# A streaming-encoder block on one core: the second up-projection phase as one chunk of 1024 tokens with halves of 512 columns, weights loaded and right factors built in the stages before

## The chip, the cores and the metric

The kernel runs on one core of a Trainium2 chip. The metric is the device time of one execution in microseconds. A core has TensorE (PE; its weight loads are listed apart as PEld), VectorE (DVE), ScalarE (ACT), GpSimd (POOL) and SyncE (SP), which here issues all DMAs in one queue. Every engine works its instructions off in a fixed order, and a waiting instruction holds up what stands behind it on its engine.

## What is computed

One layer on 2048 tokens of width 1024 with 16 learned meta tokens ahead of them: a norm, one input projection for two head groups (stick-breaking attention and a gated recurrence), one output projection with a residual, and then the part that the change touches:

```python
hn2 = rmsnorm(h, norm2_g[layer])
ug = causal_dwconv(hn2 @ w_ffn_in[layer], ffn_conv_w[layer], ffn_conv_b[layer])
u, g = jnp.split(ug, [D_FF], axis=-1)
h = h + (jax.nn.silu(g) * u) @ w_ffn_out[layer]
```

`w_ffn_in` is 1024 x 5632, `w_ffn_out` 2816 x 1024, all in float32. Each float32 factor is split in a rounded high part and the remainder, and a product is three matmuls (high by high, high by low, low by high).

## The kernel before

**Stages.** The program goes through the input projection and the recurrence, then attention, then stage C (`token_tile` and `turn2`, 17 steps: output projection, residual, second norm, transpose; the normed tokens are written to the DRAM tensor `hnT`), and stage D. Stage D goes over the tokens in two phases of 1024. In each phase `ffn_in(jf, ph)` is called for the 22 tiles `jf` of 128 columns of both halves of `w_ffn_in`, and its gated result is stored in `pd`; then `ffn_out(q)` is called for two quarters of 512 tokens, each over the 22 tiles of `w_ffn_out`, with eight accumulators in the eight PSUM banks.

**ffn_in.** The up-projection of a chunk is a 2 x 2 block product by a scheme with seven products in place of eight. Left factors: `weights(jf)` loads two tiles `wst`, forms four sums on DVE (lines 836 to 839) and splits seven factors: the high part by a copy on ACT, the low part by a subtraction on POOL (`split`, lines 704 and 705). They lie in nine rotating buffers `wt`. Right factors: `build(ch, kk, ...)` loads four blocks of `hnT` (line 717), forms four differences on DVE (line 719) and splits seven blocks into `bH` and `bL`, both on ACT and DVE. A chunk is 512 tokens, so that its blocks have 256 columns (258 in the first chunk, which has a halo of four tokens); two chunks are worked side by side, each with banks X, V and Y, and `both` runs every product for one chunk and then for the other. A product is 4 x 3 matmuls (line 851). Copies on ACT (`snap`, line 873) and additions on DVE (`plus`, line 879) make the results from the banks; then come the convolution, the gate, and a DMA to `pd` (lines 897 to 911).

**Where factors are made.** The factors of the first chunk are built during stage C (line 802), those of the second chunk at the start of stage D, those of the third and fourth between `ffn_out(1)` and the second phase (lines 941 and 942). The staging tiles of a build are the tiles `c0` and `c1` (two buffers each), which are also the results of `ffn_in` and the output rows of `ffn_out`. `wst` (four buffers) belongs to the pool of stage D.

**Order.** The tile framework simulates the program as it is written and sets each engine's order by that, so that work of one call can stand among that of the calls around it.

Of the kernel before, what the change touches and what calls it, by code (L numbers as in the profile page):

```python
# [16 lines left out]
P = 128  # L17
META = 16
# [3 lines left out]
KD = D // P  # L22
HEADS = 8
HD = 64
NT = SEQ // P
DFF = 2816
KF = DFF // P
# [4 lines left out]
HALO = 4  # L32
CHW = 512
PHW = 2 * CHW
# [21 lines left out]
def hymba_block(  # L56
# [650 lines left out]
    def half_of(ch):  # L707

        return (META - HALO, (CHW + HALO) // 2) if ch == 0 else (META + ch * CHW, CHW // 2)

    def build(ch, kk, mp, tmp):

        c0, nh = half_of(ch)
        b0, b1 = tmp()
        bt = [t[:, c * nh:(c + 1) * nh] for t in (b0, b1) for c in range(4)]
        for n, a, h in ((B11, 0, 0), (B12, 0, 1), (B21, 1, 0), (B22, 1, 1)):
            nc.sync.dma_start(bt[n], hnT[:, kk + 4 * a, c0 + h * nh:c0 + (h + 1) * nh])  # L717
        for o, a, b in ((T1, B12, B11), (T3, B22, B12), (T2, B22, T1), (T4, B21, T2)):
            nc.vector.tensor_tensor(bt[o], bt[a], bt[b], op=ALU.subtract)  # L719
        H = mp.tile([P, 7, (CHW + HALO) // 2], F32R, name=f"bH{ch % 2}{kk}", tag=f"bH{kk}")[:, :, :nh]  # L720
        L = mp.tile([P, 7, (CHW + HALO) // 2], F32R, name=f"bL{ch % 2}{kk}", tag=f"bL{kk}")[:, :, :nh]
        for d0, d1, t, m in ((0, 4, b0, 4), (4, 7, b1, 3)):
            split(H[:, d0:d1], L[:, d0:d1], t[:, :m * nh].rearrange("p (m t) -> p m t", m=m), nc.vector)
        return H, L

    with ExitStack() as CD:
        up = pool(CD, "up", 1, side="right")
        edge = up.tile([P, 2 * KF, 2], F32, name="edge")
        mats = [[], []]

        with ExitStack() as C:
            C.enter_context(ps_tu)
# [59 lines left out]
            for i in range(NT + 1):  # L792
                if 0 < i < NT:
                    mixed(i + 1)
                if i == 0:
                    g2b = cp.tile([P, D], F32, name="g2b", bufs=1)
                hg = token_tile(i, *((mA, mB)[i % 2] if i else (mM, None)), g2b)
                if late:
                    turn2(*late)
                late = (i, hg)  # L800
                if i in (8, 10, 12, 14):
                    mats[0].append(build(0, i // 2 - 4, up, ctmp))
            turn2(*late)
        wo_stack.close()

# [7 lines left out]
        with ExitStack() as Dx:  # L813
# [10 lines left out]
            def dtmp():  # L824
                return [ctile(a) for a in range(2)]

            def weights(jf):

                wu, wg = [dp.tile([P, KD, P], F32, name="wst", tag="wst", bufs=4) for e in range(2)]
                for e, w in ((0, wu), (1, wg)):  # L830
                    m = e * KF + jf
                    nc.sync.dma_start(w, w_f[:, m * P:(m + 1) * P].rearrange("(k p) c -> p k c", p=P))
# [12 lines left out]
                return out  # L845
# [9 lines left out]
            def ffn_in(jf, ph):  # L855
                a11, s1, s2, s4, s3, a12, a22 = weights(jf)
                cu, cg = ctile(0), ctile(1)
                sides = []
                for c in range(2):
                    nh = half_of(2 * ph + c)[1]  # L860
                    x0 = 0 if ph + c == 0 else HALO + c * CHW
                    sides.append((nh, slice(x0, x0 + nh), slice(x0 + nh, x0 + 2 * nh)))
                X, V, Y = [[bank()[:, :sides[c][0]] for c in range(2)] for _ in range(3)]

                def both(ps_, wt, b, first):
                    for c in range(2):
                        product(ps_[c], wt, mats[c], b, first)

                def snap(ps_, name):
                    out = []  # L870
                    for c in range(2):
                        t = dp.tile([P, (CHW + HALO) // 2], F32, name=f"{name}{c}", tag=f"{name}{c}", bufs=1)
                        nc.scalar.copy(t[:, :sides[c][0]], ps_[c])
                        out.append(t[:, :sides[c][0]])
                    return out

                def plus(dst, s, ps_, sb):
                    for c in range(2):
                        nc.vector.tensor_tensor(dst[:, sides[c][s]], ps_[c], sb[c], op=ALU.add)

                both(X, a11, B11, True)
                p1 = snap(X, "p1")
# [11 lines left out]
                for c in range(2):  # L894
                    nc.scalar.copy(cg[:, sides[c][1]], X[c])
# [17 lines left out]
            def ffn_out(q):  # L913

                acc = [[bank() for e in range(2)] for i in range(4)]
                for jf in range(KF):
                    st = dp.tile([P, KD, P], F32, name="wst", tag="wst", bufs=4).rearrange("p k c -> p (k c)")
                    nc.sync.dma_start(st, w_fo[jf * P:(jf + 1) * P, :])
                    oH, oL, pp = [dp.tile([P, 2, 4, P], F32R, name="wt", tag="wt", bufs=9) for _ in range(3)]
                    oH, oL = [t.rearrange("p a k c -> p (a k c)") for t in (oH, oL)]  # L920
                    split(oH, oL, st, nc.gpsimd)
                    pt = dp.tile([P, PHW], F32, name="t", tag="t")[:, :512]
# [25 lines left out]

_INS = ["x", "meta_tokens", "norm1_g", "w_in", "q_norm_g", "k_norm_g", "conv_w", "conv_b",
# [20 lines left out]
```

## Time and profile before

| | |
|---|---|
| median of 3 runs | 2766.45 us (2764.97 to 2766.52) |
| the profiled execution | 2765.91 us, its span 2764.2 us |
| mean granted clock of TensorE, share of full speed | 0.976 |
| PE busy | 2580.0 us (93%) |
| PEld, DVE, ACT, POOL busy | 87%, 68%, 45%, 42% |
| matmuls of the up-projection (line 851) | 7392 |
| matmuls of the down-projection (lines 108 to 110, bank `bk`) | 2112 |

The span is the time from the first to the last record. The execution's own time is 1.7 us more. A busy share is an average over stages with different limits. Matmuls are pipelined, so their durations overlap: how fast PE goes is read from how many start in a stretch, and where it stops from the idle time that stands in brackets behind a row, with the engine or transfer that ended it. The granted clock is given as a share of full speed, 1.00 for 2.4 GHz and 0.50 for 1.2 GHz.

### The profile page before, as it was taken

Reading aid. Unit: us, or ns where it says so; the run is one execution under the profiler, and the core shown is the slowest. Engines: PE = TensorE matmul, PEld = TensorE weight load, DVE = VectorE, ACT = ScalarE, POOL = GpSimd, SP = SyncE. Lnnn points to the kernel's source line nnn. Section 1 sums busy time; section 2 is a strip of 40 time slices with the busy share of each in tenths; the row PEclk is TensorE's granted clock in tenths of the full one; section 3 lists DMA queues with packets and bytes.
Section 4 is the critical chain, followed back from the end, with each engine's and each line's share of the span. In section 5 each row is a group of like instructions: output and inputs, shape, how many; then the busy total and the mean of one; then the engine's idle time right before and its main releaser. Section 6 shows DMA issues by size and latency. Waiting matters only on the chain.

```text
span 2764.2 us, 44289 instructions
## 1 busy us (share of the span) xinstructions
PE 2580.0 (93%) x16860; PEld 2392.4 (87%) x16860; DVE 1879.9 (68%) x2162; ACT 1250.4 (45%) x2419; POOL 1162.5 (42%) x1152
## 2 busy tenths in 40 slices
PE   7999799988888888999799999999969999999999
PEld 7998799977787778788699999988859999998887
DVE  5588843269999999564687777645458677765454
ACT  4355532246666667332345454432235454543222
POOL 4455564445433220000455555344436555553443
PEclk9999999999999999999899999999989999999999
DMA  4301133243333321575422222255442222224463
GB/s 154 110 32 38 47 110 99 77 111 111 94 80 80 80 72 50 162 221 181 118 92 70 85 77 78 95 171 202 152 149 77 78 76 81 81 77 160 147 204 115
DMA packets 319179, 296.64 MB, mean 107 GB/s; under 512 B 62438, under 2 KB 273622, under 8 KB 318966
## 3 DMA queue, kind: packets, MB, share of 16 engines
q1 hardware_dynamic: 318966, 293.82, 34.9%
q8 instruction: 132, 2.16, 0.3%
q14 instruction: 81, 0.66, 0.1%
HBM read 211.68 MB, written 82.07 MB: 106 GB/s over the span
## 4 chain that ended last, share of the span: by engine, by line
PE 47%; DVE 2%; POOL 1%; issue 1%; DMA 1%; SPq 0%; ACT 0%; POOLq 0%; DVEq 0%; ACTq 0%
PE bk L851 30%; PE bk L108 6%; PE bk L109 6%; PE bk L110 6%; POOL wt L705 1%; DMA out_dram<-c 0%; DMA wst<-in_w_ffn_in_dram 0%; DVE c L719 0%; DVE ss L837 0%; SPq L717 0%; DMA t<-pd 0%; DVE bL L705 0%; DVE ss L838 0%; DVE t L906 0%; DMA c<-hnT 0%
## 5 line engine op out<-in xcount | busy, mean ns | idle before, releaser
L851 PE MATMUL bk<-bH,wt 128*128 128x256 f32 (+1 forms) x4928 | 894.2, 284 | 37.9 <-ACT bH L704 18.3
L851 PEld LDWEIGHTS bk<-bH,wt 128*128 128x128 f32 x4928 | 767.4, 191 | 41.6 <-ACT bH L704 19.8
L851 PE MATMUL bk<-bL,wt 128*128 128x256 f32 (+1 forms) x2464 | 697.6, 284 | 4.9 <-DVE bL L705 4.9
L705 POOL TENSOR_TENSOR wt<-wst,wt 128x512 fp32r<-128x512 f32 (+1 forms) x264 | 464.6, 1762 | 398.0 <-ACT wt L704 388.0
L851 PEld LDWEIGHTS bk<-bL,wt 128*128 128x128 f32 x2464 | 469.8, 191 | 6.0 <-DVE bL L705 6.0
L704 ACT CAST wt<-wst 128x512 fp32r<-128x512 f32 (+1 forms) x264 | 201.4, 766 | 565.3 <-issue 301.9
L705 DVE TENSOR_TENSOR wt<-t,wt 128x512 fp32r<-128x512 f32 x88 | 202.8, 2307 | 228.0 <-ACT wt L704 228.0
L705 POOL TENSOR_TENSOR wt<-ss,wt 128x512 fp32r<-128x512 f32 x132 | 205.0, 1556 | 233.7 <-ACT wt L704 224.7
L108 PE MATMUL bk<-wt 128*128 128x512 f32 x704 | 275.5, 393 | 10.0 <-ACT wt L704 10.0
L109 PE MATMUL bk<-wt 128*128 128x512 f32 x704 | 276.0, 392 | 0.0
L110 PE MATMUL bk<-wt 128*128 128x512 f32 x704 | 271.6, 389 | 0.0
L580 DVE TENSOR_TENSOR_SCAN kp<-kp 128x456 f32<-128x456 f32 (+6 forms) x144 | 238.5, 1657 | 0.9
L612 PE MATMUL v<-tL,dv 128*128 128x256 f32 (+1 forms) x648 | 178.9, 301 | 43.2 <-DVE tL L586 42.0
L571 ACT ACTIVATE kp<-m 128x388 f32<-128x388 f32 (+13 forms) x360 | 169.1, 508 | 70.3 <-PE m L570 39.6
L906 DVE SCALAR_TENSOR_TENSOR t<-c,fw,t 128x1024 f32<-128x1024 f32 x88 | 132.5, 1506 | 78.3 <-ACT t L905 78.3
L612 PEld LDWEIGHTS v<-tL,dv 128*128 128x128 f32 x648 | 125.7, 194 | 58.9 <-DVE tL L586 57.2
L108 PEld LDWEIGHTS bk<-wt 128*128 128x128 f32 x704 | 133.6, 190 | 38.3 <-ACT wt L704 10.4
L908 DVE SCALAR_TENSOR_TENSOR c<-c,fw,t 128x1024 f32<-128x1024 f32 x88 | 160.5, 1824 | 3.0
L109 PEld LDWEIGHTS bk<-wt 128*128 128x128 f32 x704 | 133.6, 190 | 27.6
L110 PEld LDWEIGHTS bk<-wt 128*128 128x128 f32 x704 | 132.2, 188 | 27.6
L569 PE MATMUL m<-K,q 128*128 128x452 f32 (+12 forms) x360 | 143.1, 399 | 2.5 <-ACT kp L571 2.2
L563 POOL MEMSET kp<- 128x112 f32 x128 | 23.6, 190 | 284.9 <-PE t L97 130.8
(302 smaller groups left out, 5745.0 us busy)
## 6 DMA issues: line engine op xcount, KB each, us to landing
wst<-in_w_ffn_in_dram SPq DMA_DIRECT2D x88, 512.0 KB, 4.0
wst<-in_w_ffn_out_dram SPq DMA_DIRECT2D x88, 512.0 KB, 3.9
pd<-c SPq DMA_DIRECT2D x44, 512.0 KB, 2.7
t<-pd SPq DMA_DIRECT2D x88, 256.0 KB, 3.5
q<-qd SPq DMA_DIRECT2D x128, 128.0 KB, 2.8
wst<-in_w_in_dram SPq DMA_DIRECT2D x48, 192.0 KB, 2.7
xt<-in_x_dram SPq DMA_DIRECT2D x16, 512.0 KB
od<-qn SPq DMA_DIRECT2D x128, 64.0 KB, 2.1
```

What stands on the lines that cost most here:

```text
L108: nc.tensor.matmul(ps, lhsT=sH, rhs=mH, start=first, stop=False)
L109: nc.tensor.matmul(ps, lhsT=sH, rhs=mL, start=False, stop=False)
L110: nc.tensor.matmul(ps, lhsT=sL, rhs=mH, start=False, stop=last)
L569: nc.tensor.matmul(zt[:rn, :sz], lhsT=q2[:, 0, qc:qc + rn], rhs=K2[:, c0:c0 + sz], start=True, stop=False)
L571: nc.scalar.activation(kp[:rn, c0:c0 + sz], zt[:rn, :sz], AF.Sigmoid, scale=-0.125)
L580: nc.vector.tensor_tensor_scan(rev, rev, rev, initial=kp[:rn, hi:hi + 1], op0=ALU.mult, op1=ALU.bypass)
L612: nc.tensor.matmul(av[:, q0:q0 + nn], lhsT=dv[:pp, s].rearrange("p a d -> p (a d)"), rhs=tt[:pp, c:c + nn], start=(s == 0 and half == 0), ...
L704: nc.scalar.copy(h, src)
L705: low.tensor_tensor(l, src, f(h), op=ALU.subtract)
L851: nc.tensor.matmul(ps_, lhsT=s, rhs=m, start=first and k == 0 and n_ == 0, stop=k == 3 and n_ == 2, skip_group_check=True)
L906: nc.vector.scalar_tensor_tensor(t, c_[:, HALO - 1:HALO - 1 + PHW], pf[:, 1:2], t, op0=ALU.mult, op1=ALU.add)
L908: nc.vector.scalar_tensor_tensor(c_[:, uv], c_[:, uv], pf[:, 0:1], t, op0=ALU.mult, op1=ALU.add)
```

## The change

The second phase becomes one chunk of 1024 tokens whose blocks have 512 columns, with one set of banks X, V, Y: half as many matmuls, each twice as wide. The first phase keeps its two chunks. All right factors lie in two tiles, `mb0` and `mb1`, as large as before; in the second phase each holds two of the four `kk`. They are built during `ffn_out(1)`: `between(jf)` calls a build at the tiles 2, 6, 10 and 14. A build there uses all four buffers of `c0` and `c1`. `wst` moves to a pool that is open from stage C on, and the weights of the first two tiles are loaded in stage C. In the first tile of the first phase all work of the first chunk is written ahead of that of the second. `wt` has ten buffers in place of nine. The seven products, the convolution and the down-projection stay.

```diff
+    HW0 = (CHW + HALO) // 2
+    PHASES = (((META - HALO, HW0), (META + CHW, CHW // 2)), ((META + PHW, CHW),))
...
+        H, L = store
+        for n, t in enumerate(bt):
+            m = min(7 - n * per, per)
+            d = slice(n * per * nh, (n * per + m) * nh)
+            split(H[:, d], L[:, d], t[:, :m * nh], nc.vector)
...
+        wst = pool(CD, "wst", 1, side="right")
+        mb = [up.tile([P, 8 * 7 * HW0], F32R, name="mb0")]
...
+                if i == NT:
+                    staged = [stage_in(jf) for jf in range(2)]
...
-                    wt = dp.tile([P, 2, 4, P], F32R, name="wt", tag="wt", bufs=9)
+                    wt = dp.tile([P, 2, 4, P], F32R, name="wt", tag="wt", bufs=10)
...
-                X, V, Y = [[bank()[:, :sides[c][0]] for c in range(2)] for _ in range(3)]
+                X, V, Y = [[bank()[:, :s_[0]] for s_ in sides] for _ in range(3)]
+
+                apart = ph == 0 and jf == 0
+                queue = []
+
+                def run(job):
+                    for c in range(len(sides)):
+                        if apart:
+                            queue.append((c, job))
+                        else:
+                            job(c)
...
-            for ph in range(2):
-                if ph:
-                    mats[0] = [build(2, kk, up, dtmp) for kk in range(4)]
-                mats[1] = [build(2 * ph + 1, kk, up1, dtmp) for kk in range(4)]
-                for jf in range(KF):
-                    ffn_in(jf, ph)
-                for q in range(2):
-                    ffn_out(2 * ph + q)
+            mb.append(up1.tile([P, 8 * 7 * CHW // 2], F32R, name="mb1"))
+            mats[1] = [right(mb[1], PHASES[0][1], kk, 4) for kk in range(4)]
+            for jf in range(KF):
+                ffn_in(jf, 0, staged.pop(0) if staged else stage_in(jf))
+            ffn_out(0, [], lambda jf: None)
+            mats[0] = []
+
+            def between(jf):
+                if jf in (2, 6, 10, 14):
+                    kk = len(mats[0])
+                    mats[0].append(right(mb[kk // 2], PHASES[1][0], kk, 2))
+
+            ffn_out(1, [], between)
+            for jf in range(KF):
+                ffn_in(jf, 1, stage_in(jf))
+            for q in (2, 3):
+                ffn_out(q, [], lambda jf: None)
```

**What it moves in the engines' orders.** DVE at the start of stage D. `sT` is the last transposed tile of stage C, `ss` the sums of the weights, `c` a staging tile of the builds, `bL` the low parts of right factors. Before:

```order
L785 COPY sT<-u 128x512
L719 TENSOR_TENSOR c_14745<-c_14746,c_14745 128x256
L719 TENSOR_TENSOR c_14746<-c_14745,c_14746 128x256
L719 TENSOR_TENSOR c_14746<-c_14745 128x256
L719 TENSOR_TENSOR c_14746<-c_14745,c_14746 128x256
L719 TENSOR_TENSOR c_14761<-c_14762,c_14761 128x256
L705 TENSOR_TENSOR bL_14756<-c_14745,bH_14755 128x4x256
```

And with the change:

```order
L812 COPY sT<-u 128x512
L861 TENSOR_TENSOR ss<-wst 128x512
L862 TENSOR_TENSOR ss<-ss,wst 128x512
L864 TENSOR_TENSOR wst<-wst 128x512
L863 TENSOR_TENSOR ss<-wst,ss 128x512
L720 TENSOR_TENSOR c_14750<-c_14751,c_14750 128x256
L720 TENSOR_TENSOR c_14751<-c_14750,c_14751 128x256
```

The sums of the first tile's weights now stand ahead of the builds of the second chunk; before they stood behind eleven instructions of the builds.

DVE in `ffn_out(1)`, after the accumulators of `ffn_out(0)` have been read out. `wt<-t` is the low part of a tile from `pd`, one per `jf`; `mb` holds right factors. Before, 18 of these stood in one row:

```order
L705 TENSOR_TENSOR wt<-t,wt 128x512 x18
```

And with the change:

```order
L705 TENSOR_TENSOR wt<-t,wt 128x512 x2
L705 TENSOR_TENSOR mb_13216<-c_20868,mb_13216 128x1024
L720 TENSOR_TENSOR c_20869<-c_20871,c_20868 128x512
L705 TENSOR_TENSOR wt<-t,wt 128x512
L720 TENSOR_TENSOR c_20870<-c_20869,c_20871 128x512
L720 TENSOR_TENSOR c_20870<-c_20869 128x512
L705 TENSOR_TENSOR mb_13216<-c_20869,mb_13216 128x1024
L720 TENSOR_TENSOR c_20871<-c_20868,c_20870 128x512
L705 TENSOR_TENSOR mb_13216<-c_20870,mb_13216 128x1024
L705 TENSOR_TENSOR mb_13216<-c_20871,mb_13216 128x512
L705 TENSOR_TENSOR wt<-t,wt 128x512
```

This is the first of four builds; the 32 instructions of all four stand within seven steps of `jf`.

PE in the second phase, with the change. `bk_21982`, `bk_21983` and `bk_21984` are X, V and Y of the third tile, `bk_21840` and `bk_22124` X of the second and the fourth:

```order
L876 MATMUL bk_21982<-mb1_14749,wt_21959 128x512 x5
L876 MATMUL bk_21983<-mb0_13216,wt_21962 128x512 x6
L876 MATMUL bk_21983<-mb1_14749,wt_21962 128x512 x6
L876 MATMUL bk_21984<-mb0_13216,wt_21974 128x512 x6
L876 MATMUL bk_21984<-mb1_14749,wt_21974 128x512 x4
L876 MATMUL bk_21840<-mb0_13216,wt_21835 128x512 x6
L876 MATMUL bk_21840<-mb1_14749,wt_21835 128x512 x6
L876 MATMUL bk_21982<-mb0_13216,wt_21965 128x512 x6
L876 MATMUL bk_21982<-mb1_14749,wt_21965 128x512 x6
L876 MATMUL bk_21983<-mb0_13216,wt_21968 128x512 x6
L876 MATMUL bk_21983<-mb1_14749,wt_21968 128x512 x6
L876 MATMUL bk_21984<-mb1_14749,wt_21974 128x512 x2
```

Between the first product into X of a tile and the second one there are now products into V and Y and the last product of the tile before; each has 12 matmuls of 512 columns where two groups of 12 with 256 columns stood.

## Rows read from the trace of the kernel before

**Rows 1.** The page: the span, and the busy time of each engine with its instructions.

```profile
span 2764.2 us, 44289 instructions
PE 2580.0 (93%) x16860; PEld 2392.4 (87%) x16860; DVE 1879.9 (68%) x2162; ACT 1250.4 (45%) x2419; POOL 1162.5 (42%) x1152
```

**Rows 2.** Busy time by stretch, the instructions in brackets; columns in its first line.

```profile
core 0: us, PE busy (x) PEld busy (x) DVE busy (x) ACT busy (x) POOL busy (x), PEclk, DMA share, GB/s
1320.00:1370.00 50.00, 30.59 (x189) 28.59 (x189) 35.27 (x42) 19.47 (x34) 19.62 (x15) 0.73 0.47 137
1500.00:1600.00 100.00, 100.00 (x840) 100.00 (x839) 72.20 (x76) 49.05 (x90) 52.72 (x46) 1.00 0.25 80
1810.00:1910.00 100.00, 100.00 (x443) 82.84 (x442) 44.40 (x18) 29.74 (x38) 43.34 (x19) 1.00 0.48 156
2030.00:2080.00 50.00, 29.18 (x167) 25.51 (x166) 33.88 (x59) 17.83 (x25) 13.00 (x11) 0.76 0.48 148
2200.00:2300.00 100.00, 100.00 (x841) 100.00 (x840) 72.57 (x75) 49.07 (x91) 54.92 (x45) 1.00 0.25 80
```

**Rows 3.** PE's timeline at the seams of stage D: start, duration, instruction, [idle before].

```profile
1326.01 1.06 PE L97 MATMUL u<-ident,hg 128*128 128x128 f32 x4
1339.01 0.58 PE L851 MATMUL bk<-bH,wt 128*128 128x258 f32 x1 [11.95 <-ACT wt L704]
...
1791.99 0.28 PE L851 MATMUL bk<-bH,wt 128*128 128x256 f32 x1
1797.34 0.79 PE L108 MATMUL bk<-wt 128*128 128x512 f32 x1 [5.07 <-ACT wt L704]
...
2038.81 0.39 PE L110 MATMUL bk<-wt 128*128 128x512 f32 x1
2048.50 0.58 PE L851 MATMUL bk<-bH,wt 128*128 128x256 f32 x1 [9.30 <-ACT bH L704]
...
2513.32 0.28 PE L851 MATMUL bk<-bH,wt 128*128 128x256 f32 x1
2518.55 0.53 PE L108 MATMUL bk<-wt 128*128 128x512 f32 x1 [4.96 <-ACT wt L704]
```

**Rows 4.** DVE's timeline at the start of stage D.

```profile
1327.10 0.69 DVE L785 COPY sT<-u 128x512 f32<-128x512 f32 x1 [2.06 <-PE u L97]
1332.68 0.43 DVE L719 TENSOR_TENSOR c<-c,c 128x256 f32<-128x256 f32 x1 [4.89 <-DMA c<-hnT]
...
1335.23 1.22 DVE L705 TENSOR_TENSOR bL<-c,bH 128x1024 fp32r<-128x1024 f32 x1
...
1341.78 0.68 DVE L839 TENSOR_TENSOR wst<-wst 128x512 f32<-128x512 f32 x1
...
1361.14 0.94 DVE L705 TENSOR_TENSOR bL<-c,bH 128x768 fp32r<-128x768 f32 x1
```

**Rows 5.** SP's timeline there, the DMA issues of builds and weights.

```profile
1328.72 4.39 SPq L717 DMA_DIRECT2D c<-hnT  x8
1333.15 5.02 SPq L832 DMA_DIRECT2D wst<-in_w_ffn_in_dram  x4
```

**Rows 6.** Timelines of DVE, POOL and ACT in the steady down-projection, one step of `jf`.

```profile
1850.26 2.47 DVE L705 TENSOR_TENSOR wt<-t,wt 128x512 fp32r<-128x512 f32 x1 [2.98 <-ACT wt L704]
1855.70 2.47 DVE L705 TENSOR_TENSOR wt<-t,wt 128x512 fp32r<-128x512 f32 x1 [2.97 <-ACT wt L704]
...
1849.79 2.39 POOL L705 TENSOR_TENSOR wt<-wst,wt 128x1024 fp32r<-128x1024 f32 x1 [3.05 <-ACT wt L704]
...
1854.10 1.05 ACT L704 CAST wt<-wst 128x1024 fp32r<-128x1024 f32 x1 [3.87 <-issue]
```

**Rows 7.** Groups of instructions by line: count, busy us, mean ns, idle before them.

```profile
L936 DVE TENSOR_TENSOR c<-bk,c 128x512 f32<-128x512 f32 x32 | 20.7, 684 | 19.8 <-PE bk L110 19.8
```

**Rows 8.** Timelines of DVE and PE early in stage C.

```profile
1142.72 1.27 DVE L770 SCALAR_TENSOR_TENSOR hg<-ht,rstd,g2b 16x1024 f32<-16x1024 f32 x1
...
1144.04 0.42 PE L97 MATMUL t<-ident,hg 16*128 16x16 f32 x4 [0.26 <-DVE hg L770]
```

More of the change, by code (lines that the diff above doesn't have):

```diff
@@ L705, in split, with build, stores @@
         low.tensor_tensor(l, src, f(h), op=ALU.subtract)
[L707 to L715, printed above, removed]
+    HW0 = (CHW + HALO) // 2
+    PHASES = (((META - HALO, HW0), (META + CHW, CHW // 2)), ((META + PHW, CHW),))
+    def build(part, kk, store, tmp):
+        c0, nh = part
+        bt = tmp()
+        per = 8 // len(bt)
+        at = lambda n: bt[n // per][:, n % per * nh:(n % per + 1) * nh]
         for n, a, h in ((B11, 0, 0), (B12, 0, 1), (B21, 1, 0), (B22, 1, 1)):
-            nc.sync.dma_start(bt[n], hnT[:, kk + 4 * a, c0 + h * nh:c0 + (h + 1) * nh])
+            nc.sync.dma_start(at(n), hnT[:, kk + 4 * a, c0 + h * nh:c0 + (h + 1) * nh])
         for o, a, b in ((T1, B12, B11), (T3, B22, B12), (T2, B22, T1), (T4, B21, T2)):
[L719 to L724, printed above, removed]
+            nc.vector.tensor_tensor(at(o), at(a), at(b), op=ALU.subtract)
+        H, L = store
[3 more added lines that the diff above has]
+            split(H[:, d], L[:, d], t[:, :m * nh], nc.vector)
+        return [x.rearrange("p (m t) -> p m t", m=7) for x in store]
+    def stores(t, nh, n):
+        w = 7 * nh
+        return [(t[:, 2 * i * w:(2 * i + 1) * w], t[:, (2 * i + 1) * w:(2 * i + 2) * w]) for i in range(n)]
     with ExitStack() as CD:
@@ L728, in hymba_block, with stage, stage_in, stage_out @@
         edge = up.tile([P, 2 * KF, 2], F32, name="edge")
+        wst = pool(CD, "wst", 1, side="right")
+        mb = [up.tile([P, 8 * 7 * HW0], F32R, name="mb0")]
         mats = [[], []]
+        def stage():
+            return wst.tile([P, KD, P], F32, name="wst", tag="wst", bufs=4)
+        def stage_in(jf):
+            wu, wg = stage(), stage()
+            for e, w in ((0, wu), (1, wg)):
+                m = e * KF + jf
+                nc.sync.dma_start(w, w_f[:, m * P:(m + 1) * P].rearrange("(k p) c -> p k c", p=P))
+            return wu, wg
+        def stage_out(jf):
+            st = stage().rearrange("p k c -> p (k c)")
+            nc.sync.dma_start(st, w_fo[jf * P:(jf + 1) * P, :])
+            return st
         with ExitStack() as C:
@@ L801, in hymba_block @@
                 if i in (8, 10, 12, 14):
-                    mats[0].append(build(0, i // 2 - 4, up, ctmp))
+                    kk = i // 2 - 4
+                    mats[0].append(build(PHASES[0][0], kk, stores(mb[0], HW0, 4)[kk], ctmp))
+                if i == NT:
+                    staged = [stage_in(jf) for jf in range(2)]
             turn2(*late)
@@ L822, in ctile, with weights @@
                 return dp.tile([P, 2 * (CHW + HALO)], F32, name=f"c{a}", tag=f"c{a}")
[L824 to L832, printed above, removed]
+            def weights(staged):
+                wu, wg = staged
                 a11, a12, a21, a22 = wu[:, :4], wu[:, 4:], wg[:, :4], wg[:, 4:]
@@ L893, in ffn_in @@
                 both(X, a22, T4, False)
-                for c in range(2):
-                    nc.scalar.copy(cg[:, sides[c][1]], X[c])
+                run(lambda c: nc.scalar.copy(cg[:, sides[c][1]], X[c]))
+                for c, job in sorted(queue, key=lambda q_: q_[0]):
+                    job(c)
                 uv = slice(HALO - 2, HALO - 2 + PHW)
@@ L911, in ffn_in, with ffn_out @@
                 nc.sync.dma_start(pd[jf][:, ph * PHW:(ph + 1) * PHW], cu[:, uv])
-            def ffn_out(q):
+            def ffn_out(q, staged, between):
                 acc = [[bank() for e in range(2)] for i in range(4)]
                 for jf in range(KF):
-                    st = dp.tile([P, KD, P], F32, name="wst", tag="wst", bufs=4).rearrange("p k c -> p (k c)")
-                    nc.sync.dma_start(st, w_fo[jf * P:(jf + 1) * P, :])
-                    oH, oL, pp = [dp.tile([P, 2, 4, P], F32R, name="wt", tag="wt", bufs=9) for _ in range(3)]
+                    st = staged.pop(0) if staged else stage_out(jf)
+                    between(jf)
+                    oH, oL, pp = [dp.tile([P, 2, 4, P], F32R, name="wt", tag="wt", bufs=10) for _ in range(3)]
                     oH, oL = [t.rearrange("p a k c -> p (a k c)") for t in (oH, oL)]
@@ L937, in ffn_out, with right @@
                     nc.sync.dma_start(out[r0:r0 + P, :], h)
-            for ph in range(2):
-                if ph:
-                    mats[0] = [build(2, kk, up, dtmp) for kk in range(4)]
-                mats[1] = [build(2 * ph + 1, kk, up1, dtmp) for kk in range(4)]
-                for jf in range(KF):
-                    ffn_in(jf, ph)
-                for q in range(2):
-                    ffn_out(2 * ph + q)
+            def right(tile_, part, kk, n):
+                return build(part, kk, stores(tile_, part[1], n)[kk % n], lambda: [ctile(a % 2) for a in range(8 // n)])
+            mb.append(up1.tile([P, 8 * 7 * CHW // 2], F32R, name="mb1"))
[13 more added lines that the diff above has]
+                ffn_out(q, [], lambda jf: None)
 _INS = ["x", "meta_tokens", "norm1_g", "w_in", "q_norm_g", "k_norm_g", "conv_w", "conv_b",
```

24 lines of the change are left out of this document (10 added, 14 removed).

## The prediction

> **What bounds the kernel now.** The page comes first [rows 1]: PE is busy for 93% of the span, so a change pays where it gives PE fewer or cheaper matmuls or closes a gap of PE. The busy times by stretch show how PE goes in stage D [rows 2]. In the first phase 840 matmuls of 256 or 258 columns start in 100 us, in the second 841 of 256, or one every 118.9 ns; in the down-projection 443 of 512 columns, or one every 225.8 ns. In these stretches PE is busy throughout at the full clock. Two stretches stand out: 1320 to 1370 with 30.6 us of PE in 50 and a mean granted clock of 0.73, and 2030 to 2080 with 29.2 us and 0.76. PE's timeline tells what stands at the seams [rows 3]: at the first phase's start 11.95 us of idle time, at the second's 9.30 us, then short starts and stops; at the two changes to a down-projection 5.07 and 4.96 us.
>
> What a phase costs above its steady pace follows. The first phase runs from the last transposes (1326.01 + 1.06 = 1327.1) to 1792.3 [rows 3], 465.2 us; 3696 matmuls at 119.0 ns are 440.0. So **25.2 us are lost at its start**. The second runs from 2038.81 + 0.39 = 2039.2 to 2513.6, 474.4 us; 3696 at 118.9 ns are 439.5. **34.9 us are lost at its start**.
>
> **The change, part by part.** *Wider matmuls.* The second phase has 1848 matmuls of 512 columns in place of 3696 of 256. The same engine does 512 columns with three matmuls per weight split in the down-projection, at 225.8 ns [rows 2]. 1848 x 225.8 is 417.3 us against 439.5: **22.2 us less**. The bounds: the wide matmul here is at least no dearer than two narrow ones (no gain), and I see no row that would make it cheaper than 225.8. I take the row of the same width.
>
> The rows give a fixed part: 2 x 118.9 - 225.8 = 12.0 ns for every matmul saved. The Trainium skill (TensorE: Matmul & The Clock Gate, section "Wait — 56ns, not 53.3ns?") states that warm matmuls start N / 2.4 GHz + about 2.5 ns apart. By that rule joining two saves 2.5 ns, 4.6 us in all. It stands among the rivals.
>
> *Start of the second phase.* Its builds are gone from the seam, so PE waits only for the first left factor, for a bank, and for the four sums of the second tile, which stand ahead of the read-out on DVE. A read-out of a bank takes 0.68 us [rows 7]; the banks come free in the order in which they are filled, so X waits for one. I put 1 to 2 us on the bank and as much on POOL's first factors, 3 us in all, with 1 and 8 us as ends. **34.9 - 3 = 31.9 us less.** The clock goes with it: it fell to half during the idle time that disappears.
>
> *Builds inside `ffn_out(1)`.* Here the change adds. Each build has four differences of 128x512 and low parts of 1024, 1024, 1024 and 512 elements. By the nearest rows that is 4 x 0.68 + 3 x 1.22 + 0.69 = 7.1 us of DVE [rows 4], 28.3 us for four. DVE isn't free there although it is busy less than half of the time: its subtraction starts at 1850.26, POOL's at 1849.79 and ends at 1852.18, and DVE ends at 1852.73, 0.55 us later [rows 6]. The two take turns. In a step of 5.44 us they need 2.39 + 0.55 us, and 2.50 are left. The four builds stand within seven steps: 17.5 us of room. The split of a tile is done at 1855.70 + 2.47 = 1858.17, and PE, which begins a step when ACT is let go at 1854.10, needs it two steps later, at 1865.0: a lead of 6.8 us. Room and lead are 24.3 us, 4.0 short. Between builds there is a wait for the staging tiles to be loaded again; 1 us on PE in all. **5 us more**, with 0 and 18 as ends (nothing, if the waits for POOL are shorter; three reloads of 4.5 us that nothing covers besides). On SP the loads of the first build wait for the output rows to be written, with a load of `t` and one of `wst` behind them. These are needed two steps later, and the lead covers them.
>
> *Start of the first phase.* Before, SP put eight loads of blocks and then four of weights (5.02 us of issuing) into the queue [rows 5], and the first weights came so late that ACT's copy let PE go only at 1339.0 [rows 3]. Now the weights lie there, and PE can begin about 1327.5. But the second chunk is still built here, and DVE does the same work as before: from 1332.68 to 1361.14 + 0.94 = 1362.1, 29.4 us for sums, differences and low parts [rows 4]. It now begins right behind the last copy, at 1327.10 + 0.69 = 1327.8, with the four sums that need no load. So the last right factor comes at about 1358. Ahead of the matmul that needs it PE's order has 177 matmuls (84 of tile 0 for the first chunk, 48 of tile 1, 45 with parts of the second chunk), 21.1 us at 119.0 ns. The loss is at least 1358 - 1327.1 - 21.1 = 9.8 us. With the half clock at the beginning and the last factors from POOL I take 15. **10 us less**, between 0 (the order's waits eat it) and 16.
>
> *Loads in stage C.* Four loads of weights are put in, two ahead of the last stores of attention and two behind the first loads of stage C. They cost SP 5.02 / 4 = 1.25 us each [rows 5]. The loads behind them come 2.5 us later. PE's transposes at 1144.04 already waited 0.26 us for a norm that hangs on such a load [rows 8]; in the new order that norm stands ahead of another wait of DVE, which gives back about 0.7 us. **1 us more**, 0 to 4. The second pair lies ahead of a tile that is needed ten microseconds later.
>
> *Without a price.* Ten buffers for `wt`: at the changes to the down-projection the wait is for the first tile from `pd`, whose buffer the convolution holds; the gaps of 5.07 and 4.96 us stay. The copies out of the banks are as many elements as before in half as many instructions; in the second phase DVE, ACT and POOL are at 73%, 49% and 55% [rows 2] and PE hides them.
>
> **The sum.** 22.2 + 31.9 + 10 - 5 - 1 = 58.1 us. From the profiled execution's 2765.9 that leaves 2707.8, rounded **2708 us**. The median of the runs before is 2766.45, so the profiled one is 0.5 us faster than it and can stand for it.
>
> **The rivals.**
> *Builds hold up the down-projection.* DVE and POOL take turns for longer than I think, and each of the three reloads stands in the way. For it: the room is short by my own sum, and the builds follow each other without a step between. Against it: when PE stalls, POOL stalls too and leaves DVE alone. 18 us in place of 5 give 2721.
> *The start of the first phase gains nothing.* For it: DVE sets its end, and the new order puts a matmul that needs the second chunk behind only 26 of the first, so that PE may stand there. Against it: everything begins five microseconds earlier. 2718.
> *All covers hold.* No stall in `ffn_out(1)`, 16 us at the first start, 1 at the second: 2708 - 5 - 6 - 2 = 2695.
> *The wide matmul brings little.* The pair of rows would have to mislead: the up-projection reads its right factor from other tiles than the down-projection. By 2.5 ns a matmul 17.6 us of the gain are missing: 2725. Against it: the fixed part comes out of the same kernel at the same clock.
> *Slower.* With one chunk a bank is read out while only one other product runs, where there were two chunks' worth. If PE stood before the second and third product into X and the second into V of every tile, that is 66 times; 58.1 / 66 = 0.88 us each would eat the whole gain, and at 1 us it is 2774. Against it: the order puts V, Y and a product of the tile before between two products into X, and a product lasts 12 x 225.8 ns = 2.7 us.
>
> **How the numbers follow.** Forecast 2708 (2702 to 2714): 0.50. Builds hold up: 0.20. No gain at the first start: 0.12. All covers: 0.12. Little from width: 0.03. Slower: 0.03. The range reaches from 2692 to 2728: from the lowest case to the fourth, and 3 us beyond each for the ends at the second start (1 to 8) and in stage C (0 to 4). It leaves out the last case and the far end of the first. A measurement of this kernel tells 0.2% (5.5 us) from no change. Faster by more than that: 0.96; within it: 0.01; slower: 0.03.
>
> **What would show it.** In the changed profile matmuls of 512 columns in the second phase start 226 ns apart, 443 in 100 us; 238 would say that joining saves nothing. PE goes from the last down-projection matmul to the second phase with under 3 us of idle time, and the clock stays at 1.00 there. In the first `between` steps the split on DVE comes late, and PE's idle time there, released by DVE, is about 5 us. PE's first product starts at about 1328 and PE is released by ACT or DVE with right factors until about 1358. The prediction is wrong if PE shows idle time before `bk` in every tile of the second phase, or if the builds stretch `ffn_out(1)` from 120 us to over 130.

## The result, and the profile after

The changed kernel takes **2721.06 us** (median of 4 runs, 2719.19 to 2722.01) against 2765.71 us for the kernel before in the same comparison. The ratio is 0.9843, its 95% interval 0.9829 to 0.9858. The prediction was 2708 (2692 to 2728), faster: direction and range hold, the time lies 13 us above the forecast. The profiled execution took 2722.01 us, 43.9 less than the profiled one of before, where the sum said 58.1.

The page of the changed kernel, span and busy times, against [rows 1]:

```profile
span 2720.3 us, 40399 instructions
PE 2563.3 (94%) x15012; PEld 2293.5 (84%) x15012; DVE 1802.9 (66%) x2080; ACT 1241.5 (46%) x2331; POOL 1185.4 (44%) x1152
```

Its busy times by stretch, against [rows 2]:

```profile
core 0: us, PE busy (x) PEld busy (x) DVE busy (x) ACT busy (x) POOL busy (x), PEclk, DMA share, GB/s
1320.00:1370.00 50.00, 39.37 (x253) 36.99 (x251) 40.81 (x45) 22.20 (x39) 25.57 (x19) 0.80 0.39 115
1500.00:1600.00 100.00, 100.00 (x840) 100.00 (x839) 69.33 (x75) 49.07 (x90) 54.76 (x45) 1.00 0.25 80
1810.00:1910.00 100.00, 100.00 (x443) 82.81 (x442) 38.87 (x18) 28.89 (x38) 44.02 (x19) 1.00 0.48 152
1940.00:1960.00 20.00, 16.45 (x62) 13.07 (x61) 15.78 (x15) 9.91 (x13) 5.91 (x3) 0.83 0.52 168
2040.00:2060.00 20.00, 20.00 (x88) 16.24 (x88) 10.73 (x15) 7.37 (x12) 13.44 (x14) 1.00 0.61 198
2200.00:2300.00 100.00, 100.00 (x434) 81.04 (x433) 61.38 (x60) 48.71 (x72) 60.18 (x48) 1.00 0.25 79
```

Two things stand out. The second phase starts at the full clock without idle time (2040 to 2060). And in its steady part 434 matmuls stand in 100 us where the down-projection, with as many columns, has 443. A window also counts the one or two matmuls that run into it, so the starts themselves are a little further apart than the counts say. The mean distance from one start to the next, with PE's waits left out ("by starts" below), is 226.7 ns in the down-projection, **231.7** in the second phase and 119.2 in the narrow second phase of before.

PE's timeline at the seams, against [rows 3]. In the changed kernel line 876 is the product of the up-projection (851 before), 704 and 705 are the two halves of a split, 720 is a difference of a build, 861 to 864 are the sums of the weights, 906 is a copy out of a bank and 910 an addition:

```profile
1326.66 1.06 PE L97 MATMUL u<-ident,hg 128*128 128x128 f32 x4
1328.10 0.80 PE L876 MATMUL bk<-mb,wt 128*128 128x258 f32 x2 [0.38 <-ACT wt L704]
1330.64 5.29 PE L876 MATMUL bk<-mb,wt 128*128 128x258 f32 x24 [1.74 <-ACT wt L704]
1336.68 0.97 PE L876 MATMUL bk<-mb,wt 128*128 128x256 f32 x6 [0.75 <-ACT mb L704]
1339.83 2.95 PE L876 MATMUL bk<-mb,wt 128*128 128x258 f32 x12 [2.18 <-ACT p L906]
...
1784.75 3.86 PE L876 MATMUL bk<-mb,wt 128*128 128x256 f32 x31
1793.41 0.80 PE L108 MATMUL bk<-wt 128*128 128x512 f32 x1 [4.81 <-ACT wt L704]
...
2041.87 0.39 PE L110 MATMUL bk<-wt 128*128 128x512 f32 x1
2042.10 8.25 PE L876 MATMUL bk<-mb,wt 128*128 128x512 f32 x35
...
2468.43 3.06 PE L876 MATMUL bk<-mb,wt 128*128 128x512 f32 x12 [0.78 <-DVE c L910]
2474.70 0.50 PE L108 MATMUL bk<-wt 128*128 128x512 f32 x1 [3.22 <-ACT wt L704]
```

From the ends and starts of these rows and of [rows 3] the 43.9 us are accounted for:

| stretch | before | after | difference | forecast |
|---|---|---|---|---|
| up to the end of the last transposes | 1327.1 | 1327.7 | +0.7 | +1 |
| first phase | 465.2 | 460.9 | -4.3 | -10 |
| change to the down-projection | 5.1 | 4.8 | -0.3 | 0 |
| first two quarters of the down-projection | 241.9 | 248.9 | +7.0 | +5 |
| second phase, with what lies ahead of it | 474.4 | 429.2 | -45.2 | -54.1 |
| change to the down-projection | 5.0 | 3.2 | -1.7 | 0 |

### The profile page after: what moved, and what is told of

It reads as the page before. It is cut to its first block, busy times and chain, and to the rows that moved or that the text cites. A ratio compares the mean times of both kernels' runs of the same rounds, so it can differ in the third digit from the quotient of the medians.

```text
span 2720.3 us, 40399 instructions
## 1 busy us (share of the span) xinstructions
PE 2563.3 (94%) x15012; PEld 2293.5 (84%) x15012; DVE 1802.9 (66%) x2080; ACT 1241.5 (46%) x2331; POOL 1185.4 (44%) x1152
## 5 line engine op out<-in xcount | busy, mean ns | idle before, releaser
L876 PE MATMUL bk<-mb,wt 128*128 128x258 f32 (+2 forms) x5544 | 878.8, 321 | 11.5 <-ACT u L906 2.3
L876 PEld LDWEIGHTS bk<-mb,wt 128*128 128x128 f32 x5544 | 794.9, 190 | 95.4 <-DVE c L910 3.2
L705 POOL TENSOR_TENSOR wt<-wst,wt 128x512 fp32r<-128x512 f32 (+1 forms) x264 | 485.5, 1845 | 488.8 <-ACT wt L704 263.6
L705 DVE TENSOR_TENSOR wt<-t,wt 128x512 fp32r<-128x512 f32 x88 | 173.4, 1973 | 213.0 <-ACT wt L704 213.0
L705 POOL TENSOR_TENSOR wt<-ss,wt 128x512 fp32r<-128x512 f32 x132 | 197.0, 1495 | 121.7 <-ACT wt L704 120.4
L704 ACT CAST wt<-t 128x512 fp32r<-128x512 f32 x88 | 54.6, 621 | 281.2 <-PE bk L110 231.4
L940 DVE SCALAR_TENSOR_TENSOR c<-c,fw,t 128x1024 f32<-128x1024 f32 x88 | 154.0, 1750 | 3.0
L578 DVE TENSOR_TENSOR_SCAN kp<-kp,mask 128x388 f32<-128x388 f32 (+15 forms) x136 | 130.3, 968 | 0.1
```

The costliest lines, as they stand in the source:

```text
L876: nc.tensor.matmul(ps_, lhsT=s, rhs=m, start=first and k == 0 and n_ == 0, stop=k == 3 and n_ == 2, skip_group_check=True)
L940: nc.vector.scalar_tensor_tensor(c_[:, uv], c_[:, uv], pf[:, 0:1], t, op0=ALU.mult, op1=ALU.add)
```

## The experiments

Edits are against the changed kernel. The median of the kernel before lay between 2765.71 and 2767.0 us in all comparisons. The changed kernel itself was measured a second time without intent (the run with `staged = []` below, whose built program is the same): 2723.96 us against 2721.06. So a difference of less than 3 us between medians of two comparisons says nothing by itself.

### Where the right factors lie

The built program puts every weight tile `wt` and `mb0` at 32 modulo 512 bytes of a partition, but `mb1` at 192. ("Alike" below means the same place modulo 512 bytes. A block of 128, 256 or 512 columns is a multiple of 512 bytes long, so each such block lies as its tile does.) In the down-projection both factors lie in `wt` tiles. The 231 ns and 4.3 ns in the expectations are a miscount of mine: by starts it is 231.7, so 5.0 ns a matmul and 9.3 us.

```diff
-            mb.append(up1.tile([P, 8 * 7 * CHW // 2], F32R, name="mb1"))
+            mb.append(up1.tile([P, 8 * 7 * CHW // 2 + 40], F32R, name="mb1"))
```

> The changed kernel with mb1 placed 160 bytes lower in every partition (40 unused columns behind it), so that mb1, mb0 and the weight tiles wt all begin at 32 modulo 512 bytes; before this, mb1 begins at 192. No instruction moves on any engine. In the changed kernel a 512-column matmul of the second phase starts 231.0 ns after the one before it on the mean (the last start less the first, by 1847), in the down-projection 226.7. Theory place: the 4.3 ns come from where the right factors lie against the weights. It expects a pitch of 226.7 in the second phase, so 1848 x 4.3 = 8 us less there, and a few us less in the first phase, whose second chunk lies in mb1: 2706 to 2713. Rival form: the up-projection keeps one bank for 12 matmuls in a row and waits at every product for copies, and it is this that costs. It expects 231.0 ns and 2721. Rival engines: copies and additions that read banks beside the matmuls cost PE the time. It expects 2721 as well.

Measured: **2713.37 us** (2711.07 to 2715.66), ratio to before 0.981 (0.9796 to 0.9825), the lowest median of this study. Its second phase:

```profile
2200.00:2300.00 100.00, 100.00 (x443) 82.81 (x442) 63.61 (x64) 49.55 (x73) 59.71 (x46) 1.00 0.25 79
```

443 as in the down-projection, 226.7 ns by starts, and the phase is 9.3 us shorter (420.0 against 429.2). The products, the copies and all orders are the same, so the rivals form and engines fall. The first phase didn't get faster (838 to 841 matmuls of 256 and 258 columns in 100 us in all these kernels).

In the changed kernel half of the right factors, those in `mb0`, do lie like the weights. Their matmuls aren't at 226.7 ns either: from their start to the next one it is 229.8 ns, for those that read `mb1` 233.6. So the misplaced half slows the whole stretch, not its own matmuls alone.

The opposite test shifts the weight tiles against each other:

```diff
+            def wide_wt():
+                t = dp.tile([P, 8 * P + 16], F32R, name="wt", tag="wt", bufs=10)
+                return t[:, :8 * P].rearrange("p (a k c) -> p a k c", a=2, k=4)
...
-                    wt = dp.tile([P, 2, 4, P], F32R, name="wt", tag="wt", bufs=10)
+                    wt = wide_wt()
...
```

> The changed kernel with each weight tile wt made 64 bytes longer, so that the ten buffers begin at 32, 96, 160 and so on modulo 512 bytes, and the down-projection's left and right factors, both in wt, no longer lie alike. mb0 and mb1 stay where they are; the instructions are the same. Theory place: the down-projection, steady at 226.7 ns a matmul, slows to about 231: 2112 x 4.3 = 9 us more, and the second phase loses its few undisturbed matmuls, 0 to 2 us: 2728 to 2734. Rivals form and engines: nothing changes, 2721, and 226.7 ns in the down-projection.

Measured: 2730.68 us, 9.6 more. The down-projection fell from 399 matmuls in 90 us (the aligned kernel, first line) to 391, and from 226.7 to 231.1 ns by starts:

```profile
1810.00:1900.00 90.00, 90.00 (x399) 74.53 (x398) 35.25 (x17) 26.09 (x34) 39.58 (x17) 1.00 0.49 151
1810.00:1900.00 90.00, 90.00 (x391) 73.24 (x390) 35.54 (x17) 25.61 (x33) 38.57 (x16) 1.00 0.47 147
```

So wide matmuls cost 4 to 5 ns more on the mean in a stretch whose right factors and weights don't all lie alike. Since these buffers differ by multiples of 64 bytes, being alike modulo 64 isn't enough. In every stretch at 226.7 ns both factors lay at 32 modulo 512; whether being alike is what counts, or lying at 32, no run here separates.

### The width alone

```diff
-    PHASES = (..., ((META + PHW, CHW),))
+    PHASES = (..., ((META + PHW, CHW // 2), (META + PHW + CHW, CHW // 2)))
...
-            mats[0] = []
+            mats[0], mats[1] = [], []
...
-                    mats[0].append(right(mb[kk // 2], PHASES[1][0], kk, 2))
+                    for c in range(2):
+                        mats[c].append(right(mb[c], PHASES[1][c], kk, 4))
```

> The changed kernel with the second phase put back to two chunks side by side with 256 columns a block (3696 matmuls), all else kept: the eight builds of half the size stand at the same four steps of the down-projection. It prices the width alone. The prediction's term: 118.9 ns against 225.8 for twice the columns, 22 us, so 2743. By the pitch that the changed kernel shows (231.0): 3696 x 118.9 less 1848 x 231.0 = 12.6 us, so 2734. Rival, the width is worth nothing by itself: 2721 to 2724.

Measured: 2732.32 us, 11.3 more and not 22. Here the first chunk's right factors, in `mb0`, lie like the weights and the second chunk's, in `mb1`, don't. In the profiles the second phase itself takes **7.1 us** more (436.3 against 429.2) and the change behind it 1.7; the rest lies in stretches that are the same in both. With `mb1` moved as well:

> The narrow second phase with mb1 placed 160 bytes lower, so that both chunks' right factors and the weights begin at 32 modulo 512 bytes. Theory place, in its strong form: the whole 12 ns that I took for the fixed part of a matmul are costs of place, and a narrow matmul starts 113.3 ns after the one before, half of 226.7. The second phase then takes 3696 x 113.3 = 419 us, as long as with wide matmuls in this place, and the kernel is as fast as the aligned wide one within 3 us. In a weak form (place costs 4 to 5 ns, and there is a fixed part besides) 115 to 117 ns. Rival form or engines: 118.9 ns, and the time of the narrow kernel.

Measured: 2739.65 us, 7.3 us slower than the narrow kernel. Both forms of my theory fall: with both chunks alike narrow matmuls are dearer. The second phase of the two kernels, the narrow one first:

```profile
2200.00:2300.00 100.00, 100.00 (x850) 100.00 (x849) 69.47 (x76) 50.00 (x92) 55.76 (x46) 1.00 0.25 80
```

```profile
2200.00:2300.00 100.00, 100.00 (x836) 100.00 (x835) 68.96 (x75) 48.88 (x90) 57.25 (x44) 1.00 0.25 78
```

By starts 118.1 and 120.0 ns. Where all factors lie alike, 256 columns more take 226.7 - 120.0 = 106.7 ns, so 120.0 - 106.7 = 13.3 ns of a matmul don't grow with its columns. Where they don't all lie alike, the same working leaves 11.4 (the narrow kernel) to 12.5 (the kernel before) for narrow matmuls and 18.4 for the wide ones of the changed kernel. The Trainium skill (TensorE: Matmul & The Clock Gate, section "Wait — 56ns, not 53.3ns?") has about 2.5 ns on top of N / 2.4 GHz; no stretch here shows so little, and the measurement decides. A fixed part that joining saves is real, and with factors that lie alike the width is worth 23.5 us in the second phase (443.5 against 420.0).

### The builds: at the seam, spread, in other hands

```diff
-            mats[0] = []
...
-            ffn_out(1, [], between)
+            ffn_out(1, [], lambda jf: None)
+            mats[0] = [right(mb[kk // 2], PHASES[1][0], kk, 2) for kk in range(4)]
```

> The changed kernel with the four builds of the second phase behind the second down-projection, where such builds stood before the change, and none inside it. By the prediction's terms: the start of the second phase costs 31.9 us more, the down-projection 5 us less: 2748. By what the changed kernel's trace shows: 32.6 more (34.9 against 2.3 over the steady pace), 7.0 less (248.85 against 241.86 us for the first two quarters): 2747. Rival, the builds of wide blocks are cheaper at the seam than the narrow ones were (half as many instructions, one chunk to wait for): 2735 to 2740.

Measured: 2746.25 us, 25.2 more; the two quarters take 241.8 us and the second phase 462.0. Its PE starts that phase like the kernel before:

```profile
2046.17 0.80 PE L876 MATMUL bk<-mb,wt 128*128 128x512 f32 x1 [10.55 <-ACT mb L704]
2047.43 1.22 PE L876 MATMUL bk<-mb,wt 128*128 128x512 f32 x2 [0.46 <-DVE mb L705]
2050.13 4.99 PE L876 MATMUL bk<-mb,wt 128*128 128x512 f32 x12 [1.47 <-ACT mb L704]
```

The two terms of the move, 32 and 7 us, are settled by this. For what makes the 7 us, here is the one long stall of the changed kernel on four engines, behind a row of DVE that shows the low part of a `t` alone, and PE's waits for DVE in the two quarters with their sum, number and longest:

```profile
1937.15 0.68 DVE L705 TENSOR_TENSOR wt<-t,wt 128x512 fp32r<-128x512 f32 x1
...
1939.51 1.05 ACT L704 CAST mb<-c 128x1024 fp32r<-128x1024 f32 x1 [1.89 <-DMA c<-hnT]
...
1943.36 0.61 ACT L704 CAST wt<-t 128x512 fp32r<-128x512 f32 x1
...
1945.05 5.74 POOL L705 TENSOR_TENSOR wt<-wst,wt 128x1024 fp32r<-128x1024 f32 x2 [4.89 <-ACT wt L704]
...
1945.16 3.44 DVE L705 TENSOR_TENSOR mb<-c,mb 128x1024 fp32r<-128x1024 f32 x1
...
1945.80 0.61 ACT L704 CAST wt<-t 128x512 fp32r<-128x512 f32 x1
...
1948.52 2.82 DVE L705 TENSOR_TENSOR wt<-t,wt 128x512 fp32r<-128x512 f32 x1
...
1951.40 0.80 PE L110 MATMUL bk<-wt 128*128 128x512 f32 x1 [3.55 <-DVE wt L705]
```

```profile
PE bk L110 <- DVE wt L705: 4.2, 3, 3.6
```

ACT waits with a build's copy for a staging tile to be loaded again, and its copies of the tiles `t` stand behind. The low part of `t` then stands on DVE behind a low part of a build, and both take turns with POOL (3.44 and 2.82 us where they take 1.22 and 0.68 alone). ACT had the high part ready at 1945.80 + 0.61 = 1946.41; the low part began 2.1 us later and took 2.1 us longer than alone, which together is more than the stall. PE stands for 3.55 us and goes on at half the clock (0.83 on the mean from 1940 to 1960). Three runs tried to take a part of that away.

```diff
-            ffn_out(0, [], lambda jf: None)
...
-            ffn_out(1, [], between)
+            ffn_out(0, [], between((4, 13)))
+            ffn_out(1, [], between((4, 13)))
```

> The changed kernel with the four builds spread over the first two quarters of the down-projection (two in each, at the tiles 4 and 13) in place of all four in the second quarter. The place they are written to is free from the end of the first phase. Theory room: in the changed kernel PE stood once for 3.55 us and twice for under 0.5, because DVE had four builds in seven steps, and then ran at the half clock; with two builds at a time the lead of the splits covers them: 5 to 7 us less, 2714 to 2716. Rival turns: DVE and POOL take turns, so each build costs PE the same wherever it stands: 2721.

Measured: 2721.29 us, no gain. The two quarters take 247.0 us, 1.8 less; the same program gave 248.9 and 250.5 in two profiles, so a small gain there is likely and not certain. The first quarter hides its two builds, but the second still has one stall of 3.5 us in the same form: the framework puts the two builds of a quarter back to back although the code has them nine tiles apart. Then part of the low parts went to POOL:

```diff
-            split(H[:, d], L[:, d], t[:, :m * nh], nc.vector)
+            split(H[:, d], L[:, d], t[:, :m * nh], nc.gpsimd if n in pooled else nc.vector)
...
```

> The changed kernel with part of the builds' low parts on POOL in place of DVE: of the second chunk of the first phase the 768-element ones, of the second phase one of 1024 and the one of 512 in each build. Theory DVE: at the first phase's start DVE has no free time from 1330 to 1360 while POOL stands still for 10 us (1350 to 1360), and in the down-projection DVE is what PE waits for; taking 3.8 us of DVE there and 7.6 us here gives 2 to 4 us at the start and 3 to 6 in the down-projection: 2711 to 2717. Rival turns: POOL takes twice as long for the same elements and DVE waits its turn; the low parts of the weights, on POOL too, come late in their place, and PE waits for POOL: 2721 to 2730.

Measured: 2730.79 us, 9.7 more: a miss, just beyond the rival's range. The first phase lost 4.8 us and the two quarters 4.3. PE's waits in the two quarters:

```profile
PE bk L108 <- ACT wt L704: 5.5, 2, 5.0
PE bk L109 <- POOL wt L705: 3.3, 1, 3.3
PE bk L110 <- DVE wt L705: 3.1, 2, 2.4
```

> The kernel with part of the low parts on POOL and mb1 160 bytes lower (40 unused columns behind it). If place and the builds are independent, it is the run before less 7.7 us: by theory DVE 2703 to 2710, by rival turns 2713 to 2722. The second phase goes at 226.7 ns a matmul.

Measured: 2721.97 us, 8.8 less than without the 40 columns. The gain by place comes again, beside other work. Last, on the kernel with `mb1` moved, the low part of `t` in other hands:

```diff
-                    split(pH, pL, pt, nc.vector)
+                    split(pH, pL, pt, nc.gpsimd if q == 1 and jf < 16 else nc.vector)
```

> The kernel with mb1 160 bytes lower, and in the second quarter of the down-projection the low part of the tile from pd on POOL for the first 16 steps, so that no split that PE waits for stands behind a build on DVE. In the changed kernel PE stood 3.55 us for such a split (it began 2.1 us after ACT was done with the high part, behind two low parts of a build, and took 2.82 us beside POOL), then ran at the half clock for about 3 us. Theory order: the two quarters fall from 248.9 (249.8 with mb1 moved) to 242 to 244 us, and the kernel from 2713.4 to 2706 to 2709. Rival turns: POOL has 2.4 us a step already and gets 1.3 to 1.9 more, while DVE's builds take turns with it; PE then waits for POOL: 2713 or more.

Measured: 2713.88 us, the same as with `mb1` moved alone; the two quarters take 249.0 us (249.8 there). Theory order falls in its simple form. ACT and PE in this kernel:

```profile
1943.38 1.05 ACT L704 CAST mb<-c 128x1024 fp32r<-128x1024 f32 x1 [7.03 <-DMA c<-hnT]
1944.33 0.62 ACT L704 CAST wt<-t 128x512 fp32r<-128x512 f32 x1
...
1959.35 0.50 PE L108 MATMUL bk<-wt 128*128 128x512 f32 x1 [0.87 <-ACT wt L704]
1961.74 0.79 PE L110 MATMUL bk<-wt 128*128 128x512 f32 x1 [1.66 <-POOL wt L705]
```

ACT now waits 7.03 us for the reload with the copies of `t` behind it. That the reload ahead of ACT is the common root is what these traces suggest and don't show; a build whose copies don't stand ahead of those of `t` on ACT wasn't tried.

### The start of the first phase

```diff
-                apart = ph == 0 and jf == 0
+                apart = False
```

> The changed kernel (2721.06 us) with the first tile's work no longer ordered by chunk: every product runs for the first chunk and then for the second. The weights still lie there when the phase begins. In the changed kernel the first phase takes 460.9 us from the end of the last transposes, 20.9 more than its steady pace. Theory cover: the last right factor of the second chunk comes at about 1360.8 in the changed kernel, and 84 matmuls of the first chunk are what PE can do before. Without the order PE has 12 (1.4 us) and stands until all four builds are done, so the phase takes 8 to 10 us more: 2729 to 2731. Rival, the early weights alone made the gain: 2721 within 3 us.

Measured: 2723.0 us, which is no difference; the first phase takes 463.0 us, where it takes 460.8 to 461.7 in the profiles of the kernels that have it as the changed kernel. The order by chunks is worth 1 to 2 us, not 8 to 10: without it PE stands 4.71 us once, but has 180 matmuls without a wait soon after.

```diff
-                    staged = [stage_in(jf) for jf in range(2)]
+                    staged = []
```

> The changed kernel with the first two tiles' weights loaded when stage D begins, behind the loads of the builds, and no longer in stage C; the order by chunks stays. Theory cover: the first weights land about 10 us later, PE begins at about 1339 as before the change, and the last right factor is as late as in the changed kernel or later, since the sums of the weights stand ahead of the builds on DVE and wait for the load: the phase takes 4 to 12 us more, of which stage C gives back 0.6: 2725 to 2732. Rival, the chain of right factors alone sets the end and the weights don't matter: 2720 to 2722.

Measured: 2723.96 us (2718.49 to 2725.37), first phase 461.6. It didn't test what it was meant to: the built program is that of the changed kernel, instruction for instruction and address for address, since the open pool lets the loads go early wherever they are written. PE begins at 1326.89 here too. Only with the pool back in stage D are the weights late:

```diff
-        wst = pool(CD, "wst", 1, side="right")
...
-                return wst.tile([P, KD, P], F32, name="wst", tag="wst", bufs=4)
+                return dp.tile([P, KD, P], F32, name="wst", tag="wst", bufs=4)
...
-                    staged = [stage_in(jf) for jf in range(2)]
+                    staged = []
```

> The changed kernel with the weight tiles wst back in the pool of stage D, as before the change, so that no weight can be loaded before stage C ends; the order by chunks in the first tile stays. (With the loads merely written later, in the run before, they still went out early, because the pool was open.) Theory early weights: PE then begins the first phase at about 1339 in place of 1328 and loses what it did in between, 57 matmuls at the half clock and 6.4 us of waits; the phase takes 465 us or more in place of 460.9: 2725 to 2728. Theory DVE: DVE's work (sums, differences, low parts, then the sums and gates of the next tiles) sets when PE stops waiting, at about 1400, and that is as late with late weights, since DVE fills its time with the differences first: 2721 to 2723.

Measured: 2728.12 us (2723.21 to 2733.33), first phase 467.4. PE starts 12 us late and loses 6.5 in the end. That is also 2.2 us more than the kernel before took (465.2), which had late weights too; which of the other changes costs this wasn't tried.

```profile
1340.80 0.80 PE L875 MATMUL bk<-mb,wt 128*128 128x258 f32 x2 [12.37 <-ACT wt L704]
1342.35 6.42 PE L875 MATMUL bk<-mb,wt 128*128 128x258 f32 x34 [0.76 <-POOL wt L705]
...
1361.15 29.88 PE L875 MATMUL bk<-mb,wt 128*128 128x256 f32 x227 [4.03 <-DVE mb L705]
```

## Why the prediction was right, and where it was off

**Start of the second phase (31.9 less).** Right: 429.2 us are 1848 x 231.7 ns and 1.0 us, so nothing is lost there where by the same count 33.8 were (474.4 less 3696 x 119.2 ns). The 3 us for bank and first factors weren't needed. In the run with the builds at the seam the loss is there again.

**Wider matmuls (22.2 less): the step that failed.** "I take the row of the same width" put the down-projection's pace, 225.8 by count, into the up-projection. The row had the right width but not the right place: there both factors lie in `wt` tiles, here half of the right factors lie at another address modulo 512. 3696 x 119.2 less 1848 x 231.7 is 12.4 us, so 9.8 were missing. The rival "the wide matmul brings little" had said in its reason for it that the right factor is read from other tiles; it had the place right, though half of its 17.6 us. 40 unused columns bring 9.3 us back in this phase, 7.7 in the kernel's median.

**Start of the first phase (10 less, got 4.3).** The direction holds, the 15 us of remaining loss were 19.2 (460.9 less 3696 x 119.5 ns). PE in the changed kernel from the last product that waited for a right factor on:

```profile
1355.16 14.55 PE L876 MATMUL bk<-mb,wt 128*128 128x256 f32 x119 [0.44 <-DVE mb L705]
1370.78 1.85 PE L876 MATMUL bk<-mb,wt 128*128 128x258 f32 x13 [1.08 <-ACT u L906]
1372.84 9.79 PE L876 MATMUL bk<-mb,wt 128*128 128x256 f32 x80 [0.21 <-DVE c L910]
1383.97 13.13 PE L876 MATMUL bk<-mb,wt 128*128 128x256 f32 x108 [1.35 <-DVE c L910]
1398.37 1.85 PE L876 MATMUL bk<-mb,wt 128*128 128x258 f32 x13 [1.27 <-ACT u L906]
```

Up to 1355 PE stood 6.8 us, and some 60 matmuls at the half clock cost about 6 us more. Behind that it stood another 3.9 us until 1398, for sums and additions that DVE had still to catch up with; no term held these. DVE in the changed kernel, against [rows 4], and behind it a row of the kernel before:

```profile
1328.36 1.57 DVE L861 TENSOR_TENSOR ss<-wst 128x512 f32<-128x512 f32 x1
...
1333.27 2.54 DVE L720 TENSOR_TENSOR c<-c,c 128x256 f32<-128x256 f32 x2 [0.32 <-DMA c<-hnT]
...
1337.26 4.22 DVE L720 TENSOR_TENSOR c<-c,c 128x256 f32<-128x256 f32 x3
...
1359.83 0.96 DVE L705 TENSOR_TENSOR mb<-c,mb 128x768 fp32r<-128x768 f32 x1 [0.17 <-ACT mb L704]
```

```profile
1347.15 4.24 DVE L719 TENSOR_TENSOR c<-c,c 128x256 f32<-128x256 f32 x3
```

I counted the same work at the same durations, begun five microseconds earlier. DVE began 4.3 us earlier (1328.36 against 1332.68), but the last right factor came only 1.3 us earlier (1360.8 against 1362.1) and not at 1358: DVE needed 32.4 us and not 29.4. In the changed kernel three differences take 4.22 us beside POOL, where one alone takes 0.43 in [rows 4]; but such turns stood in the kernel before too (4.24), and differences and sums together took 21.0 us against 20.0. The rest of the 3 us are three more additions ahead of the last low part (1.3 us) and 0.6 us more of waits.

**Builds inside the down-projection (5 more, got 7.0).** Right in kind: DVE and ACT are late and PE waits 4.2 us, 3.55 of it once. The half clock behind that stall wasn't in the sum. The reload that I put at 1 us stands at the head of the stall; what it costs by itself no run shows.

**Stage C (1 more, got 0.7).** In the kernels of this study whose work up to there is the same, PE's first product starts anywhere from 1326.20 to 1330.01, so this term isn't told from nothing. The change to the last down-projection gained 1.7 us that I had put at nothing.

The time is that of the rival "builds hold up the down-projection" (2721), but not by its mechanism: the builds took 7 us, not 18; the missing 14 are 9.8 of width, 5.7 of the first start and 2 of builds, less 3 gained elsewhere. That three misses together stay inside the range is in part luck: the largest belongs to a case that had got a chance of 0.03.

## What to carry to other kernels

A pace taken from another stage holds only if the operands lie alike: before costing a wider matmul by such a row, compare the addresses of right factors and weights, and measure a padding of some columns, which adds no instruction (here it made wide matmuls faster and narrow ones slower). Work moved under a busy stage is priced by what stands behind it on each in-order queue (a copy that waits for a reload, then a subtraction in turn with POOL), and PE's waits of 4.2 us cost 7.0 here, because the clock fell behind them. An earlier start is no gain in full: a chain on DVE that began 4.3 us earlier ended 1.3 us earlier.

## What the runs showed of the hardware

The mean start-to-start time of matmuls depends on where their operands lie. In stretches where the right factors and the weights all lay alike modulo 512 bytes of a partition it was 226.7 ns for 512 columns and 120.0 for 256. In stretches where half of the right factors or more lay otherwise than the weights it was 231.1 to 232.2 and 118.1 to 119.2. So the same padding makes wide matmuls faster and narrow ones slower, by 9.3 and 7.2 us in this phase. Why, whether it is being alike that counts or the place 32 at which all alike tiles lay, and whether 512 is the smallest such number (64 isn't enough), stays open.
